# Four projection units computed block by block, convolution rows kept on chip, and tail loads issued one step ahead

## The chip, the cores and the metric

The kernel runs on one core of a Trainium2 chip. A core has TensorE (PE: matmuls into PSUM banks of 128 x 512 float32, with a separate weight-load part, PEld), VectorE (DVE), ScalarE (ACT), GpSimd (POOL) and SyncE (SP), which here only issues transfers. Each engine works off its own queue in order; an instruction that waits holds up all that stand behind it on that engine. Transfers are issued from the queues of SP, ACT and POOL. The metric is the device time of one execution in microseconds; the profile's times count from the start of the profiled span.

## The reference

One decoder layer on x of 2048 tokens by 1024 channels, float32:

```
hn   = rms_norm(x, mix_pre_g)
proj = hn @ w_in                        # q 512, k 128, v 128, u 1024 columns
a, gate = split(u)                      # 512 columns each
h    = a * sigmoid(gate)
h    = causal depthwise conv of width 31 over tokens (h) + bias
h    = silu(layer_norm(h))              # over the 512 channels
conv = h @ w_conv_pw
attn = sliding-window attention(q, k, v), window 128, sinks, position bias
x    = x + rms_norm(concat(attn, conv) @ w_out, mix_post_g)
ff   = (silu(rms_norm(x) @ w_gate) * (rms_norm(x) @ w_up)) @ w_down
out  = x + rms_norm(ff)
```

## The kernel before, in words

**Numbers.** Every float32 matmul is made of three: each operand is split into a high part (a rounded copy, made by ACT) and a low part (the rest, made by a subtraction on DVE or POOL), and `three` (L188) adds high x high, high x low and low x high. The low parts of weights are stored to a scratch tensor (`lo_in`, `lo_out`) the first time and read back for later token tiles (`split_w`, L129, argument `made`).

**Tiling.** The tokens are cut into four tiles of 512 (t = 0 to 3 in the code; tile 1 to 4 in the text). For each tile the stages are: A, the input projection, in 14 units of 128 output columns; B, attention, in blocks of 128 tokens; T, the 31 taps of the convolution on DVE; C, the tail of the convolution (transpose, layer norm, swish, transpose back); W, the output projection with its norms and residual. Then F and G compute the FFN for tiles 1 and 2 together and later for tiles 3 and 4. J multiplies `w_conv_pw` into the lower half of `w_out` once (`w_join`), so that W has eight row groups: four of attention, four of convolution.

**A projection unit.** `proj(u)` (L334) loads 512 KB of weights (all eight blocks of 128 input channels for 128 columns), splits them in two halves and runs 8 x 3 matmuls into one PSUM bank. For t = 0 the input is not normalized first: x is only scaled by its channel gain and split, and the norm's reciprocal, one number per token, is multiplied in behind the projection. It comes from `sum_squares` (ACT squares, DVE additions) and `norm_x` (four small matmuls with ones, some 13 short DVE steps, four transposes into a row `rb`). Until `rb` stands, units 0 and 1 of tile 1 hold their banks. `glu` then makes the gated product of two units, stores it to `glu_scr`, and the taps read it from there. The low parts of the weights of units 0 to 5 (`TAPS0`) are made on POOL. `FILL` and `NWARM` are matmuls on the identity that nobody reads, issued ahead of and between the first unit's.

**The convolution tail.** `stage_tail` (L594) loads four rows of 128 channels from `y_scr`, each right before its transpose, into tiles of the tag `fc`, of which there are three, shared with the taps. `conv_tail` (L609) makes mean and variance, waits a planned time (`YL`, `YL2`), scales, transposes back through the single bank `ct`, applies swish (two ACT passes, one DVE) and stores four rows to `mixT`. Stage W loads them from there (L766) and splits them.

**The order of the work.** The order is written by a planner in the code. The main stage yields an amount of planned time for each piece (5.2 for a projection unit), and lanes (`Lane`, L1333) fill in their pieces at a set rate per planned time: `lb` attention, `lc` taps (rates 0.7 for T0, 1.1 for T1), `ld` J and the tails C0 and C1 (rate 2), `lw` W0, later C2, W2, C3, W3 (rate 1.25). The taps of a channel group may be planned once its GLU store is. A scheduler then orders each engine's queue by these priorities and its own model of durations.

Of the kernel before, what the change touches and what calls it, by code (L numbers as in the profile page):

```python
# [12 lines left out]
F32 = mybir.dt.float32  # L13
# [12 lines left out]
P = 128  # L26
# [8 lines left out]


@with_exitstack
def layer_kernel(ctx, tc, x, xT, cols, rows, sinks, relb, onehot, w_in, w_pw, w_out, w_gate, w_up, w_down, out):
# [162 lines left out]
    NCOL = cols.shape[1]  # L201
    colt = cst.tile([P, NCOL], F32, name="colt")
    nc.sync.dma_start(colt, cols)
    w0 = t_("raw", (P, 2, T))
    x0 = []
    for i in range(4):
        xt = f4("x", (P, 2, T))
        for j in range(2):
            if i == 0:
                nc.sync.dma_start(w0[:, j], w_in[0, :, j * T : (j + 1) * T])  # L210
            nc.sync.dma_start(xt[:, j], xT[2 * i + j, :, 0:T])
# [116 lines left out]
    def stage_a(t, hn, before_kv, hooks, post=None):  # L328
        L = f"A{t}"
        lab[0] = L  # L330
        raw0 = [w0 if t == 0 else None]
        rb = None

        def proj(u):  # L334
            w = kweight(u, t > 0, raw0.pop() if raw0 else None)
            o = mm()
            for k in range(KC):
                three(o, [(w[k], (hn[k][:, 0], hn[k][:, 1]))], k == 0, k == KC - 1)
                for _ in range(FILL[k] if t == u == 0 else 0):
                    mat(warm[:, 0:P], ident, ident, start=True, stop=True)  # L340
            return o

        def step(u):
            if u in hooks:
# [19 lines left out]
            yield  # L364

        for c in range(4):
            og = proj(2 * c)
            if post and c == 0:
                yield 5.2
                step(0)  # L370
                late = og, proj(1)
                next(post)
                yield 5.2
                step(1)
                continue
# [7 lines left out]
            half.send(proj(2 * c + 1))  # L383
            yield 5.2
            step(2 * c + 1)
        before_kv()
# [204 lines left out]
            nc.sync.dma_start(y_scr[c, :, t * T : (t + 1) * T], y)  # L591
            yield 0.68

    def stage_tail(t):  # L594
        L = f"C{t}"
        lab[0] = L
        yt = t_("yt", (P, 4, 4 * P))
        ycs = []
        turn = turner(yt, ycs)
        for c in range(4):  # L600
            lab[0] = L
# [5 lines left out]
        yield from conv_tail(t, yt)  # L607

    def conv_tail(t, yt):  # L609
# [12 lines left out]
        for s in range(4):  # L622
            act(yt[:, s], yt[:, s], AF.Identity, scale=r[:, s : s + 1], bias=nmr[:, s : s + 1])
        for c in range(4):
            b = ct()
            for s in range(4):
                nc.tensor.transpose(b[:, s * P : (s + 1) * P], yt[:, s, c * P : (c + 1) * P], ident)
            th = f2("fc")
            act(th, b, AF.Tanh, scale=lnh[:, c : c + 1], bias=lnh[:, 4 + c : 5 + c])
            v = f2("fc")  # L630
            act(v, b, AF.Identity, scale=ln_g[:, c : c + 1], bias=ln_b[:, c : c + 1])
            stt(v, th, 1.0, v, ALU.add, ALU.mult)
            nc.sync.dma_start(mixT[4 + c, :, t * T : (t + 1) * T], v)
            yield 2
            lab[0] = L

# [108 lines left out]
    def stage_w(w, spill, G, atag, htag, mtag, bank_of, norm=None):  # L745
        L = f"W{w}"
        lab[0] = L
        acc = [f4(atag) for _ in range(4)]

        def acts(gi, ms=None):  # L750
            aa = []
            for m in ms or load(gi):
                a = hl(htag)
                act(a[:, 0], m, AF.Copy)  # L754
                vtt(a[:, 1], m, a[:, 0].bitcast(F32), ALU.subtract)
                aa.append([a])
            return aa

        stage = spare_tile() if w == 1 else None

# [12 lines left out]
            lab[0] = L  # L773
        nxt = acts(0, first)
        for gi in range(KC // G):
            aa = nxt
            for n in range(2):
                lab[0] = L
                if n == 0 and gi + 1 < KC // G:
# [4 lines left out]
                if n == 1 and gi + 1 < KC // G:  # L784
# [5 lines left out]
        tail = norm_w(w, spill, acc, mtag, gb)  # L790
        if norm:
            norm(tail)
        else:
            yield from tail

    def norm_w(w, spill, acc, mtag, gb):
        L = f"W{w}"
# [768 lines left out]
```

## Time and profile before

| | us |
|---|---|
| median of 3 runs | 1939.36 (1937.44 to 1939.98) |
| the profiled execution | 1939.64 |
| its span, first to last instruction | 1937.9 |
| TensorE busy | 1898.4 |
| VectorE busy | 1487.0 |
| ScalarE busy | 970.7 |
| GpSimd busy | 228.2 |

The page also says that 443.56 MB were moved, 229 GB/s on average, and that the granted TensorE clock was 0.994 of full speed over the span. In the views, a row names the source line, the engine, the operation and "out<-in" by the program's tile names with the stage behind the @ sign (A, B, C, F, G, H, J, W; X is the start). In brackets or behind the last bar stands how long the engine was idle before the instruction and what ended that. Most matmuls have line L108 and most DVE instructions L85, which are helpers; there the tile names tell the work. A matmul's own duration contains its latency, so PE's real pace is read from many matmuls in a row.

### The profile page before, as it was taken

The page shows a single profiled execution, that of the slowest core. Times are in us where ns is not written, and L with a number is a line of the kernel's source. Part 1 is how long each engine was busy: PE and PEld are TensorE (multiplying, and loading weights), DVE is VectorE, ACT ScalarE, POOL GpSimd, SP SyncE. Part 2 cuts the span into 40 slices and gives each one's busy share as a digit, 9 for nine tenths or more (in the row PEclk, how much of TensorE's full clock was granted, in tenths as well). Part 3 has the DMA queues.
Part 4 walks back from the last instruction along what each step waited for, and adds up shares of the span by engine and source line. Part 5 has one row for each costly group of instructions (what it writes and reads, how often), then busy time and mean ns, then how long its engine had stood idle before and what let it go on. Part 6 is the DMA issues. An engine that isn't in the chain of part 4 may idle for free.

```text
span 1937.9 us, 26778 instructions
## 1 busy us (share of the span) xinstructions
PE 1898.4 (98%) x8730; PEld 1536.7 (79%) x8730; DVE 1487.0 (77%) x2747; ACT 970.7 (50%) x1910; POOL 228.2 (12%) x327
## 2 busy tenths in 40 slices
PE   9999999999999999999999999999999999999997
PEld 7877776777778878878888778888888888888886
DVE  5999889897875899888988676787566665455557
ACT  5355444657666533334445565586534343345443
POOL 6000100221010000000000020010033333211000
PEclk9999999999999999999999999999999999999999
DMA  8897656679868676877396788699544443376664
GB/s 318 273 318 231 226 170 183 199 227 318 275 213 281 222 255 219 278 251 253 127 325 222 239 288 298 221 348 328 188 161 155 160 156 107 130 246 190 208 194 154
DMA packets 229181, 443.56 MB, mean 229 GB/s; under 512 B 22920, under 2 KB 48688, under 8 KB 229040
## 3 DMA queue, kind: packets, MB, share of 16 engines
q1 hardware_dynamic: 207408, 406.19, 63.4%
q10 hardware_dynamic: 19392, 28.32, 4.0%
q0 software_dynamic: 2240, 7.34, 1.0%
q8 instruction: 68, 1.11, 0.2%
q14 instruction: 73, 0.60, 0.1%
HBM read 320.64 MB, written 121.12 MB: 228 GB/s over the span
## 4 chain that ended last, share of the span: by engine, by line
PE 73%; DVE 10%; DMA 10%; issue 2%; ACT 2%; POOL 2%; SPq 0%; DVEq 0%; ACTq 0%; POOLq 0%
PE mm@F L108 35%; PE mm@G L108 18%; PE mm@A L108 7%; PE mm@W L108 4%; DVE fc@C L85 4%; PE tr@W L108 3%; PE tr@B L108 2%; DMA raw@A<-w_in 2%; PE ct@J L108 1%; DMA td<-fc@G 1%; DVE w@F L85 1%; PE tr@B L514 1%; DMA fc@G<-w_down 1%; DMA td<-wx@G 1%; DMA mids<-fa@F 1%
## 5 line engine op out<-in xcount | busy, mean ns | idle before, releaser
L85 DVE SCALAR_TENSOR_TENSOR fc@C<-glu@C,colt,fc@C 128x512 f32<-128x512 f32 x480 | 354.2, 754 | 2.6
L108 PE MATMUL mm@F<-hl@H,w@F 128*128 128x512 f32 x1056 | 254.2, 389 | 1.2 <-ACT mm@F L1000 1.2
L108 PEld LDWEIGHTS mm@F<-hl@H,w@F 128*128 128x128 f32 x1056 | 198.1, 188 | 42.8 <-ACT mm@F L1000 1.6
L108 PE MATMUL mm@G<-hl@G,hl@G 128*128 128x512 f32 x924 | 223.9, 393 | 1.6 <-ACT hl@G L846 1.0
L846 ACT ACTIVATE w@F<-chl@F 128x512 fp32r<-128x512 f32 x220 | 135.6, 625 | 150.5 <-PE mm@F L108 140.6
L108 PE MATMUL mm@A<-hl@A,w@A 128*128 128x512 f32 x840 | 203.7, 394 | 1.6 <-DVE hl@A L85 1.0
L108 PEld LDWEIGHTS mm@G<-hl@G,hl@G 128*128 128x128 f32 x924 | 171.7, 188 | 38.0 <-ACT hl@G L846 1.4
L108 PE MATMUL mm@G<-w@G,hl@G 128*128 128x512 f32 x876 | 199.5, 389 | 0.0
L108 PEld LDWEIGHTS mm@G<-w@G,hl@G 128*128 128x128 f32 x876 | 164.4, 188 | 34.1
L108 PEld LDWEIGHTS mm@A<-hl@A,w@A 128*128 128x128 f32 x840 | 155.8, 188 | 39.4 <-DVE hl@A L85 2.3
L85 DVE TENSOR_TENSOR w@F<-chl@F,w@F 128x512 fp32r<-128x512 f32 x198 | 146.1, 742 | 35.7 <-ACT w@F L846 35.3
L108 PE MATMUL mm@F<-ql@H,w@F 128*128 128x512 f32 x528 | 129.9, 391 | 2.6 <-ACT w@F L846 2.6
L108 PE MATMUL mm@F<-mid@H,w@F 128*128 128x512 f32 x528 | 130.7, 391 | 0.0
L108 PE MATMUL mm@F<-p@H,w@F 128*128 128x512 f32 x528 | 130.6, 393 | 0.0
L108 PE MATMUL mm@F<-x@H,w@F 128*128 128x512 f32 x528 | 128.3, 391 | 0.0
L108 PEld LDWEIGHTS mm@F<-ql@H,w@F 128*128 128x128 f32 x528 | 98.6, 188 | 23.2 <-ACT w@F L846 3.0
L108 PEld LDWEIGHTS mm@F<-p@H,w@F 128*128 128x128 f32 x528 | 100.2, 190 | 21.2 <-ACT at@F L1104 0.2
L108 PEld LDWEIGHTS mm@F<-mid@H,w@F 128*128 128x128 f32 x528 | 99.5, 189 | 21.0 <-ACT fa@F L1111 0.3
L108 PEld LDWEIGHTS mm@F<-x@H,w@F 128*128 128x128 f32 x528 | 98.4, 188 | 22.1 <-DVE mid@W L85 0.8
L133 ACT ACTIVATE w@A<-raw@A 128x512 fp32r<-128x512 f32 x110 | 67.6, 626 | 79.6 <-PE mm@A L108 50.8
L85 DVE TENSOR_TENSOR w@G<-raw@G,w@G 128x512 fp32r<-128x512 f32 x73 | 51.3, 703 | 68.5 <-ACT w@G L846 67.2
L108 PE MATMUL tr@W<-w@W,ql@W 128*128 128x512 f32 x384 | 96.9, 396 | 3.8 <-ACT ql@W L754 2.7
(307 smaller groups left out, 3185.7 us busy)
## 6 DMA issues: line engine op xcount, KB each, us to landing
mids<-fa@F SPq DMA_DIRECT2D x154, 256.0 KB, 2.8
raw@A<-w_in SPq DMA_DIRECT2D x55, 512.0 KB, 4.6
w@A<-lo_in SPq DMA_DIRECT2D x84, 256.0 KB, 3.6
fc@G<-mids SPq DMA_DIRECT2D x77, 256.0 KB, 3.4
fa@G<-mids SPq DMA_DIRECT2D x75, 256.0 KB, 5.1
w@W<-lo_out SPq DMA_DIRECT2D x48, 256.0 KB, 5.5
chl@F<-w_gate SPq DMA_DIRECT2D x22, 512.0 KB, 3.9
raw@F<-w_gate SPq DMA_DIRECT2D x22, 512.0 KB, 3.6
```

Of the source, the lines that this page charges most:

```text
L85: r = op(*args, **kw)
L108: r = nc.tensor.matmul(*args, **kw)
L133: act(w[:, 0], raw, AF.Copy)
L514: nc.tensor.transpose(o[:, i * P : (i + 1) * P], pr[:, 4 * g + i], ident)
L846: act(w[:, 0], x, AF.Copy)
```

## The change

1. *First four units.* A new input `w_four` holds the columns of units 0 to 3 by blocks of 128 input channels. For t = 0 the blocks of x and of `w_four` are loaded alternately, and `four` runs one block at a time through four banks: split on ACT and DVE, a store of the low part on POOL, twelve matmuls. The second half of the norm and the first two GLUs come behind unit 4; units 4 and 5 use banks of the tag `tr`. All low parts of input weights are made on DVE. `FILL` has 3 such matmuls instead of 11, and the bank for these matmuls is `ct`.
2. *Tiles 3 and 4.* The tail of the convolution is no longer a lane item of its own. W2 and W3 run its first half, then the attention rows, then its second half, whose rows are split on the spot (`operand`) and used by the projection; they are neither stored to nor loaded from `mixT`.
3. *Tails of tiles 1 and 2.* The load of a row is issued before the transpose of the row ahead of it, with a planned 2 behind the first.

```diff
     def kweight(u, made, raw=None):
-        hs = weight(w_in[u].rearrange("p (a b) -> p a b", a=2), lo_in[u], made, raw, u < TAPS0)
+        hs = weight(w_in[u].rearrange("p (a b) -> p a b", a=2), lo_in[u], made, raw, False)
...
     for i in range(4):
         xt = f4("x", (P, 2, T))
+        wt = f4("p", (P, 2, T))
         for j in range(2):
-            if i == 0:
-                nc.sync.dma_start(w0[:, j], w_in[0, :, j * T : (j + 1) * T])
             nc.sync.dma_start(xt[:, j], xT[2 * i + j, :, 0:T])
+            for cs in (slice(0, T // 2), slice(T // 2, T)) if i + j == 0 else (slice(0, T),):
+                nc.sync.dma_start(wt[:, j, cs], w_four[2 * i + j, :, cs])
         x0.append(xt)
+        w0 += [wt[:, 0], wt[:, 1]]
...
+        def four():
+            os = [mm() for _ in range(4)]
+            for k in range(KC):
+                lab[0] = L
+                w = hl("w")
+                for cs in (slice(0, T // 2), slice(T // 2, T)) if k == 0 else (slice(0, T),):
+                    act(w[:, 0, cs], w0[k][:, cs], AF.Copy)
+                    vtt(w[:, 1, cs], w0[k][:, cs], w[:, 0, cs].bitcast(F32), ALU.subtract)
+                nc.gpsimd.dma_start(
+                    lo_in[0:4, k // 4, :, k % 4 * P : (k % 4 + 1) * P].rearrange("u p c -> p u c"),
+                    w[:, 1].bitcast(F32).rearrange("p (u c) -> p u c", c=P))
+                for u in range(4):
+                    us = slice(u * P, (u + 1) * P)
+                    three(os[u], [((w[:, 0, us], w[:, 1, us]), (hn[k][:, 0], hn[k][:, 1]))], k == 0, k == KC - 1)
+                for _ in range(FILL[k]):
                     mat(warm[:, 0:P], ident, ident, start=True, stop=True)
+                if k == KC - 2:
+                    next(post)
+                yield 2.7
+                if k % 2:
+                    step(k // 2)
+            return os
...
         for c in range(4):
-            og = proj(2 * c)
             if post and c == 0:
-                yield 5.2
-                step(0)
-                late = og, proj(1)
-                next(post)
-                yield 5.2
-                step(1)
+                os = yield from four()
+            if post and c < 2:
                 continue
-            if post and c == 1:
+            og = proj(2 * c, tr if post and c == 2 else mm)
+            if post and c == 2:
                 rb = next(post)
-                next(glu(0, *late))
+                for j in range(2):
+                    next(glu(j, *os[2 * j : 2 * j + 2]))
...
+        if t < 2:
+            row(0)
+            yield 2
         for c in range(4):
-            y = f2("fc")
-            nc.sync.dma_start(y, y_scr[c, :, t * T : (t + 1) * T])
-            ycs.append(y)
+            row(c + (t < 2))
             turn(c)
             yield 0.5
...
             stt(v, th, 1.0, v, ALU.add, ALU.mult)
-            nc.sync.dma_start(mixT[4 + c, :, t * T : (t + 1) * T], v)
+            if sink:
+                sink(v)
+            else:
+                nc.sync.dma_start(mixT[4 + c, :, t * T : (t + 1) * T], v)
...
+        def operand(m):
+            a = hl(htag)
+            act(a[:, 0], m, AF.Copy)
+            vtt(a[:, 1], m, a[:, 0].bitcast(F32), ALU.subtract)
+            return [a]
...
+        conv = []
+        tail = stage_tail(w, lambda v: conv.append(operand(v))) if w > 1 else ()
+        for y in tail:
+            if y == YL2:
+                break
+            yield y
...
         for gi in range(KC // G):
-            aa = nxt
+            if w > 1 and G * gi == 4:
+                yield from tail
+                lab[0] = L
+            aa = nxt if w < 2 or G * gi < 4 else conv[G * gi - 4 : G * gi - 4 + G]
...
-    FILL = (2, 2, 2, 2, 2, 1, 0, 0)
+    FILL = (1, 1, 1, 0, 0, 0, 0, 0)
...
-    warm = mm()
+    warm = ct()
...
-    lw.add("C2", stage_tail(2))
     lw.add("W2", stage_w(2, True, 2, "mid", "ql", "at", tr))
-    lw.add("C3", stage_tail(3), lambda: since(lc, "T3", CS))
-    lw.add("W3", stage_w(3, True, 2, "mid", "ql", "at", tr, norm=lambda g: lw.add("N3", g)))
+    lw.add("W3", stage_w(3, True, 2, "mid", "ql", "at", tr, norm=lambda g: lw.add("N3", g)),
+           lambda: since(lc, "T3", CS))
```

More of the change, by code (lines that the diff above doesn't have):

```diff
@@ L37, in layer_kernel @@
 @with_exitstack
-def layer_kernel(ctx, tc, x, xT, cols, rows, sinks, relb, onehot, w_in, w_pw, w_out, w_gate, w_up, w_down, out):
+def layer_kernel(ctx, tc, x, xT, cols, rows, sinks, relb, onehot, w_in, w_four, w_pw, w_out, w_gate, w_up, w_down, out):
     nc = tc.nc
@@ L330, in stage_a, with proj @@
         lab[0] = L
[L331 removed]
         rb = None
[L334 to L336 removed]
+        def proj(u, bank_of=mm):
+            w = kweight(u, t > 0)
+            o = bank_of()
             for k in range(KC):
                 three(o, [(w[k], (hn[k][:, 0], hn[k][:, 1]))], k == 0, k == KC - 1)
[L339 to L341 removed]
+            return o
+        def four():
[13 more added lines that the diff above has]
+                for _ in range(FILL[k]):
+                    mat(warm[:, 0:P], ident, ident, start=True, stop=True)
+                if k == KC - 2:
[4 more added lines that the diff above has]
+            return os
         def step(u):
@@ L382, in stage_a @@
             step(2 * c)
-            half.send(proj(2 * c + 1))
+            half.send(proj(2 * c + 1, tr if post and c == 2 else mm))
             yield 5.2
@@ L599, in stage_tail, with row, conv_tail @@
         turn = turner(yt, ycs)
+        def row(c):
+            if c < 4:
+                lab[0] = L
+                ycs.append(f2("fc"))
+                nc.sync.dma_start(ycs[c], y_scr[c, :, t * T : (t + 1) * T])
+        if t < 2:
+            row(0)
+            yield 2
         for c in range(4):
-            lab[0] = L
-            y = f2("fc")
-            nc.sync.dma_start(y, y_scr[c, :, t * T : (t + 1) * T])
-            ycs.append(y)
+            row(c + (t < 2))
             turn(c)
             yield 0.5
-        yield from conv_tail(t, yt)
-    def conv_tail(t, yt):
+            lab[0] = L
+        yield from conv_tail(t, yt, sink)
+    def conv_tail(t, yt, sink):
         L = f"C{t}"
@@ L748, in stage_w @@
         acc = [f4(atag) for _ in range(4)]
-        def acts(gi, ms=None):
[L751 to L757, printed above, removed]
+        def operand(m):
[3 more added lines that the diff above has]
+            return [a]
+        def acts(gi, ms=None):
+            return [operand(m) for m in ms or load(gi)]
+        conv = []
[4 more added lines that the diff above has]
+            yield y
+        lab[0] = L
         stage = spare_tile() if w == 1 else None
@@ L775, in stage_w @@
         for gi in range(KC // G):
-            aa = nxt
+            if w > 1 and G * gi == 4:
+                yield from tail
+                lab[0] = L
+            aa = nxt if w < 2 or G * gi < 4 else conv[G * gi - 4 : G * gi - 4 + G]
             for n in range(2):
                 lab[0] = L
-                if n == 0 and gi + 1 < KC // G:
+                more = gi + 1 < KC // G and (w < 2 or G * gi + G < 4)
+                if n == 0 and more:
                     if w < 2 and G * gi + G == 4:
@@ L783, in stage_w @@
                     rows_next = load(gi + 1)
-                if n == 1 and gi + 1 < KC // G:
+                if n == 1 and more:
                     nxt = acts(gi + 1, rows_next)
@@ L789, in stage_w @@
                 yield from block_half(acc, list(zip(aa, ws)), n, gi == 0, L, bank_of)
-        tail = norm_w(w, spill, acc, mtag, gb)
+        last = norm_w(w, spill, acc, mtag, gb)
         if norm:
-            norm(tail)
+            norm(last)
         else:
-            yield from tail
+            yield from last
     def norm_w(w, spill, acc, mtag, gb):
@@ L1551 @@
         ("w_in", kblocks(wi)),
+        ("w_four", cc(wi[:, 0 : 4 * P].reshape(KC, P, 4 * P))),
         ("w_pw", cc(wp)),
```

5 lines of the change are left out of this document (2 added, 3 removed).

## The prediction

> **What bounds the kernel now.** I read the page's first lines, then the stretches of time, then the groups and waits of the stretches that the change touches.
>
> ```profile
> span 1937.9 us, 26778 instructions
> PE 1898.4 (98%) x8730; PEld 1536.7 (79%) x8730; DVE 1487.0 (77%) x2747; ACT 970.7 (50%) x1910; POOL 228.2 (12%) x327
> ```
>
> TensorE (PE) is the bound: it is idle for 39.5 us of 1937.9, and a change that leaves its matmuls alone can gain only from that idle time, from half-clock time, and from stretches in which PE counts as busy but issues few matmuls. The view of stretches shows where these lie (columns: stretch, its length, then busy time and number of instructions of PE, PEld, DVE, ACT, POOL, then granted clock, DMA share, GB/s).
>
> ```profile
> 0.00:5.00 5.00, 3.35 (x15) 3.35 (x16) 0.54 (x7) 1.91 (x2) 1.20 (x8) 1.00 0.50 122
> 5.00:10.00 5.00, 4.34 (x29) 3.63 (x27) 1.50 (x2) 2.90 (x4) 3.85 (x4) 1.00 1.00 305
> 10.00:15.00 5.00, 4.40 (x17) 2.91 (x17) 4.74 (x9) 4.75 (x8) 0.00 (x0) 1.00 1.05 404
> 15.00:20.00 5.00, 4.62 (x20) 3.30 (x19) 4.64 (x4) 3.25 (x5) 3.94 (x4) 1.00 1.03 415
> 20.00:40.00 20.00, 18.58 (x87) 15.08 (x86) 11.93 (x26) 10.77 (x18) 12.89 (x17) 1.00 0.86 313
> 40.00:60.00 20.00, 20.00 (x86) 15.43 (x85) 16.31 (x28) 4.89 (x9) 12.33 (x18) 1.00 0.89 296
> 60.00:200.00 140.00, 137.99 (x679) 108.44 (x678) 136.07 (x297) 77.32 (x183) 8.22 (x16) 1.00 0.81 275
> 200.00:260.00 60.00, 57.23 (x299) 44.03 (x298) 49.73 (x115) 23.51 (x64) 9.63 (x4) 1.00 0.63 208
> 1060.00:1070.00 10.00, 7.57 (x37) 5.80 (x35) 6.36 (x10) 4.37 (x8) 0.00 (x0) 1.00 0.70 213
> 1070.00:1080.00 10.00, 9.67 (x35) 7.59 (x36) 9.69 (x16) 6.42 (x12) 0.00 (x0) 0.83 0.46 138
> ```
>
> Three things are to be seen. The first 20 us issue only 81 PE instructions while the DMA rings are full from 5 us on. From 60 to 200 us PE and DVE are both full (138.0 and 136.1 of 140): there DVE is almost a second bound. At 1060 to 1080 PE stands still for 2.8 us and then runs at a lower clock.
>
> **Part 1, the first four units together.** Now unit 0 waits, block by block, for all of x, and each later unit waits for its own 512 KB of weights. The groups of the first 40 us:
>
> ```profile
> L108 PE MATMUL mm@A<-hl@A,w@A 128*128 128x512 f32 x110 | 28.1, 402 | 1.6 <-DVE hl@A L85 1.0 <-ACT hl@A L319 0.6
> L135 POOL TENSOR_TENSOR w@A<-raw@A,w@A 128x512 fp32r<-128x512 f32 x9 | 11.9, 1339 | 12.9 <-ACT w@A L133 12.8
> L85 DVE TENSOR_TENSOR gb@A<-gb@A,wx@A 128x512 f32<-128x512 f32 x6 | 8.8, 1463 | 1.7 <-ACT wx@A L283 1.5
> L108 PE MATMUL mm@X<-ident 128*128 128x128 f32 x40 | 7.2, 347 | 1.6 <-POOL ident masks.py:199 1.6
> L133 ACT ACTIVATE w@A<-raw@A 128x512 fp32r<-128x512 f32 x10 | 5.9, 624 | 3.3 <-DMA raw@A<-w_in 3.3
> L85 DVE SCALAR_TENSOR_TENSOR hl@A<-x@X,colt,hl@A 128x512 fp32r<-128x512 f32 x8 | 5.7, 748 | 5.4 <-ACT hl@A L319 5.4
> L319 ACT ACTIVATE hl@A<-x@X,colt 128x512 fp32r<-128x512 f32 x8 | 5.3, 711 | 2.0 <-DMA x@X<-xT 2.0
> L108 PE MATMUL ct@A<-ones,gb@A 128*128 128x1 f32 x8 | 0.9, 239 | 0.0
> L283 ACT ACTIVATE wx@A<-x@X 128x1024 f32<-128x1024 f32 x4 | 4.2, 1049 | 4.0 <-DVE gb@A L85 4.0
> ```
>
> and from the timeline, in order, PE, ACT and SP:
>
> ```profile
> 31.33 11.61 PE L108 MATMUL mm@A<-hl@A,w@A 128*128 128x512 f32 x50
> 4.31 0.63 ACT L133 ACTIVATE w@A<-raw@X 128x512 fp32r<-128x512 f32 x1 [2.22 <-DMA raw@X<-w_in]
> 6.19 0.72 ACT L319 ACTIVATE hl@A<-x@X,colt 128x512 fp32r<-128x512 f32 x1 [1.25 <-DMA x@X<-xT]
> 8.46 0.72 ACT L319 ACTIVATE hl@A<-x@X,colt 128x512 fp32r<-128x512 f32 x1 [0.77 <-DMA x@X<-xT]
> 1.73 0.42 SPq L211 DMA_DIRECT2D x@X<-xT  x1
> 2.67 3.78 SPq L211 DMA_DIRECT2D x@X<-xT  x7
> ```
>
> At full pace a matmul takes 11.61/50 = 0.23 us, a unit of 24 5.5 us. 110 are done by 40 us, so the 96 of four units end at 40 - 14 x 0.23 = 36.8 us.
>
> After: each step k needs 256 KB of x and 256 KB of weights and gives PE 12 matmuls, 2.75 us. The rings moved 0.61 MB by 5 us, 2.13 MB by 10 us and 4.15 MB by 15 us (5 x 122, 305, 404 GB/s). Step 0 with its constants is 0.6 MB, step 1 ends at 1.1 MB (6.7 us), step 7 at 4.3 MB (15.3 us). Landing is seen later than moving: the second x block stood at 1.1 MB of what was issued and was used at 8.46, so I add 1.7 us. Step 0 can start at about 6.2 (first operand used at 6.19), step 1 at 8.4 plus one ACT and one DVE pass over x, 8.4 + 0.71 + 0.75 = 9.9; step 7's data are there by 17 us, when PE is at step 3. From step 1 PE is the limit: 9.9 + 7 x 2.75 + 0.9 (the sums' ones matmuls) = 30.0 us. ACT gives 0.71 + 0.62 + 0.52 (half a square) = 1.85 us a step. DVE gives 0.75 for x, and for the low part of the weights and the sum two tensor_tensor, each 0.74 by this row of the page:
>
> ```profile
> L85 DVE TENSOR_TENSOR w@F<-chl@F,w@F 128x512 fp32r<-128x512 f32 x198 | 146.1, 742 | 35.7 <-ACT w@F L846 35.3
> ```
>
> 2.23 us, also under 2.75. The sums stand at 1463 ns now, twice that, because they ran beside POOL's splits; these leave POOL. **Gain 36.8 - 30.0 = 6.8 us.** At best step 1 starts right behind step 0 (9.0): 7.7. At worst each in-order step waits once as now (0.5 us a step): 2.8.
>
> The rest of part 1. SP issues 18 transfers instead of 10 ahead of x of the next tile, 8.5 us at 0.47 each, before the last byte is due. Fewer fillers (24 of today's 40 records) cost nothing if PE waits no longer than 0.9 us at step 1. POOL issues eight stores of the low parts instead of the splits and is free for it; their pieces are shorter (512 B), which no row prices: 0 if they land at leisure (tile 2 reads them after 90 us), up to 1 us if the rings, full until 20 us, are slowed. I take 0. The banks of units 0 to 3 stay held until the norm is there, but units 4 and 5 use three other banks, so the first taken bank is wanted 11 us after step 7; each pair is read in two DVE passes of 0.75 with one of 0.62 on ACT between, 4 us for both pairs behind a norm that stands behind unit 4 (5.5). I take 0, at worst 2.
>
> **Part 2, what DVE pays.** Units 4 and 5 are split on DVE, 4 x 0.74 = 3.0 us, where 60 to 200 us is full. The taps of the convolution start when the first GLU is stored; the planner now reaches it after 21.6 + 5.2 units of its clock instead of 15.6 (10.4 relative to the end of tile 1). On the chip the first tap stood at
>
> ```profile
> 44.30 0.54 DVE L85 TENSOR_SCALAR fc@C<-glu@C,colt 128x512 f32<-128x512 f32 x1
> 463.70 0.32 SPq L766 DMA_DIRECT2D mb@J<-mixT  x1
> 472.12 1.31 ACT L754 ACTIVATE hl@W<-mb@J 128x512 fp32r<-128x512 f32 x2 [2.03 <-PE mm@A L108]
> DMA to landing us min/median/max: 2.3/4.8/7.9
> ```
>
> which is 13 us behind the norm (unit 4's matmuls start behind its transposes, at 31.33). Now the norm's transposes stand behind unit 4, 30.0 + 5.5, and POOL, with no splits ahead of the GLU's last product, saves one pass of 1.3: 47.2. With PE 6.8 us ahead, taps and splits are 6.8 + 2.9 + 3.0 = 12.7 us later against PE. 200 to 260 us has 10.3 us of DVE idle time to make that up. Who would wait is the projection of tile 2 for its convolution rows: they were loaded at 463.70 (landed about 468.5, median 4.8) and used at 472.12 behind PE, 3.6 us of slack. **Cost taken: 1.5 us**; ends 0 (all made up) and 9.1 (12.7 less the slack); it lies near the low end, since idle time and slack together, 13.9, cover the slip.
>
> **Part 3, rows of tiles 3 and 4 on chip.** Sixteen transfers of 256 KB go (eight stores, eight loads). What they cost at 1060 to 1090:
>
> ```profile
> ACT ql@W L754 <- DMA at@W<-mixT: 17.8, 3, 8.9
> PE tr@W L108 <- ACT ql@W L754: 2.7, 1, 2.7
> 1070.33 3.81 PE L108 MATMUL tr@W<-w@W,ql@W 128*128 128x512 f32 x9 [2.69 <-ACT ql@W L754]
> ```
>
> ACT stands before the load up to 8.9 us, and PE once for 2.7; behind it the clock is 0.83 for 10 us, 1.7 us more. 4.4 us in all. The copies and subtractions stay. Next late is the conv tail itself (ACT, DVE, one bank), which runs while the attention rows' matmuls and the other lane feed PE. **Gain 4.0**; ends 4.4 and -1.0 (a new wait of 2.7 us at both tiles). The planner's wait of 20 units goes too, so both tiles end earlier, which nobody waits for.
>
> A rule weighed here: the Trainium skill, TensorE: Matmul & The Clock Gate, Part 1, lets the clock fall only after an idle window of about 3.4 us. By it the 2.7 us wait costs no clock and this part would gain 2.7 instead of 4.4; this trace disagrees, with 0.83 behind a wait of 2.69 us.
>
> **Part 4, tails of tiles 1 and 2.** The one wait seen:
>
> ```profile
> 399.47 0.66 PE L575 MATMUL ct@C<-ident,fc@C 128*128 128x128 f32 x4 [1.67 <-DMA fc@C<-y_scr]
> ```
>
> The row is now issued about a step earlier. **Gain 1.0**; ends 1.7 and 0 (three buffers, still one behind the taps).
>
> **Sum.** 6.8 - 1.5 + 4.0 + 1.0 = 10.3 us. The profiled execution took 1939.64 (span 1937.9 and 1.7 around it), 0.3 above the median 1939.36 of the three runs: 1929.3, so 1929.0 on the median.
>
> **Rivals.** *The start is fed no better*: ACT and DVE take their work in an order in which PE waits at each step. For it: PE waited on both for 1.6 us of unit 0's 24 matmuls; against: 2.75 us of matmuls per step now cover what 0.7 did not. Gain 2.8 instead of 6.8 and the DVE cost half: 1933; with two more us lost on the held banks 1935.
>
> *The conv tail stalls PE in place of the load*: -1.0 instead of 4.0, 1934. For it: one bank and four passes over ACT and DVE per row; against: ACT is half idle there (4.4 and 6.4 of 10).
>
> *Slower: the late taps starve the projection of tile 2.* If the taps follow the planner's clock and not free DVE time, 10.4 units later is much more on the chip: from 320 to 460 us tile 4's projections got
>
> ```profile
> L108 PE MATMUL mm@A<-mid@A,w@A x132: 387/389/628, 320.9 to 459.7; 128*128 128x512 f32 x132
> L108 PE MATMUL mm@A<-hl@A,w@A x126: 387/389/504, 319.8 to 459.9; 128*128 128x512 f32 x126
> ```
>
> 258 matmuls, 10.75 units of 5.2 in 140 us, 2.5 us each, so up to 26 us. Less 3.6 of slack PE waits 22: 1939.4 - 11.8 + 22 = 1950. It decides once the slip is over 11.8 + 3.6 = 15.4 us. Against: DVE's 10.3 us of idle time, and a slip by its own work of 12.7 us.
>
> The Trainium skill's clock rule (same page) speaks against fewer fillers: a window without matmuls halves the clock. By the sum the longest wait at the start is 0.9 us, so I give it no case.
>
> **How the numbers follow.** My case 0.58 (1924 to 1933 by its own ends); start no better 0.15 (half of it inside 0.2%); conv stall 0.12; starved projection 0.15. A measurement tells about 0.2%, 3.9 us, from no change. Faster: 0.58 + 0.12 + 0.08 = 0.78, same 0.07, slower 0.15. The range 1921 to 1938 leaves out the slow rival and a little of my own case below: ends of 7.7, 0, 4.4 and 1.7 give 1925.6, and waits elsewhere that move with the new order may take or give some 4 us.
>
> **What would show it.** Right: 96 matmuls of the first units done near 30 us; tile 1's projections ending 6 to 7 us earlier; no ACT wait on loads of mixT after 900 us and PE without a wait over 1 us at 1040 to 1100, clock 1.00; no wait of ct@C on y_scr. Wrong: PE waiting near 460 to 530 us on the convolution rows of tile 2, a clock below 1 in the first 30 us, or new PE waits on ql@W.

## The result, and the profile after

| | before | after |
|---|---|---|
| median | 1939.67 (6 runs, 1935.90 to 1945.08) | 1958.46 (6 runs, 1951.05 to 1959.09) |
| ratio, 95% interval | | 1.0073 (1.0055 to 1.0091) |
| profiled execution, span | 1939.64, 1937.9 | 1959.09, 1957.3 |
| granted TensorE clock | 0.994 | 0.990 |

Slower by 0.7%, 14 us, by the ratio on record, in which the experiments below are given too (the two medians alone are 18.8 us apart). 10 us less had been forecast: 1929.0, in a range of 1921 to 1938. On other chips the median of the kernel before lay between 1942 and 1946, so the experiments are given as ratios to its runs on the same chip.

The first lines of the page, after:

```profile
span 1957.3 us, 26728 instructions
PE 1904.8 (97%) x8714; PEld 1539.7 (79%) x8714; DVE 1490.0 (76%) x2760; ACT 971.6 (50%) x1911; POOL 206.9 (11%) x311
```

TensorE is busy for 6 us more although it has 16 matmul records less, which is time at half clock, and it is idle for 13 us more (52.5 against 39.5). DVE has 3 us more work in sum: thirteen more passes for low parts of weights (some 9.4 us, since those of units 0 to 3 came to DVE too, not only the four of units 4 and 5 that the prediction put down as a load), against 4.6 us less in the norm's six sums. POOL has 21 us less.

The stretches of time, after (columns as in the prediction):

```profile
10.00:15.00 5.00, 5.00 (x23) 4.14 (x23) 4.21 (x8) 4.95 (x8) 1.95 (x3) 1.00 1.05 402
15.00:20.00 5.00, 5.00 (x23) 4.13 (x23) 5.00 (x9) 4.10 (x7) 1.83 (x3) 1.00 1.05 397
20.00:40.00 20.00, 20.00 (x95) 16.32 (x94) 9.74 (x31) 9.10 (x16) 2.68 (x8) 1.00 1.03 400
40.00:60.00 20.00, 18.01 (x68) 13.38 (x67) 14.39 (x25) 6.17 (x11) 5.53 (x12) 0.91 0.83 278
60.00:200.00 140.00, 130.97 (x641) 103.94 (x640) 124.89 (x281) 71.52 (x175) 9.54 (x16) 0.98 0.74 251
200.00:260.00 60.00, 60.00 (x303) 46.31 (x302) 52.65 (x119) 26.16 (x69) 5.09 (x4) 1.00 0.67 212
385.00:450.00 65.00, 60.25 (x304) 45.71 (x301) 55.15 (x132) 34.99 (x84) 12.15 (x24) 0.97 0.67 207
450.00:640.00 190.00, 180.19 (x870) 139.74 (x869) 131.14 (x288) 121.51 (x254) 20.30 (x56) 0.97 0.76 259
1060.00:1070.00 10.00, 10.00 (x47) 8.28 (x46) 6.12 (x12) 4.19 (x9) 0.00 (x0) 1.00 0.62 193
1070.00:1080.00 10.00, 10.00 (x46) 8.27 (x45) 7.68 (x19) 5.49 (x10) 3.75 (x12) 1.00 0.70 210
```

The two ends of the change look as forecast: from 10 to 40 us PE is full at clock 1.00, and the wait at 1067 us is gone. The loss lies between them. From 60 to 200 us, PE issues 38 instructions fewer than before (641 against 679), although DVE, the second bound there, is busy for 11 us *less* (124.9 against 136.1). From 385 to 640 us PE loses more, against these rows of before:

```profile
385.00:450.00 65.00, 63.33 (x320) 47.43 (x319) 55.51 (x126) 39.16 (x92) 13.22 (x34) 1.00 0.73 226
450.00:640.00 190.00, 185.78 (x925) 146.76 (x924) 149.61 (x317) 132.09 (x276) 17.62 (x47) 1.00 0.80 271
```

Busy time is 3.1 + 5.6 us less, and a clock of 0.97 in place of 1.00 over these 255 us costs some 7.7 us more: 16 us in all. I counted the matmuls of the projections in the traces and set the end of each unit (24 matmuls; 14 units a tile; the end is the start of the last one plus 0.23 us) side by side:

| end of unit | before | after | difference |
|---|---|---|---|
| 4 | 36.9 | 30.4 | -6.5 |
| 7 | 54.0 | 51.4 | -2.6 |
| 25 | 169.7 | 165.2 | -4.5 |
| 28 | 189.3 | 196.0 | +6.8 |
| 48 | 391.5 | 396.7 | +5.2 |
| 50 | 425.1 | 435.7 | +10.5 |
| start of the third row group of H | 616.8 | 637.8 | +21.0 |

So the front's gain is there and is given back twice over: 11 us at the step from tile 2 to tile 3 (units 25 to 28), and 16 us between 390 and 640 us. PE's own waits name the places; after, the five largest of 0 to 190 us, then all of 385 to 430 us:

```profile
PE mm@A L108 <- DVE ql@A L85: 4.7, 1, 4.7
PE mm@A L108 <- DVE w@A L85: 1.8, 1, 1.8
PE tr@B L108 <- POOL p@B L535: 1.7, 1, 1.7
PE ct@X L108 <- POOL ident masks.py:199: 1.7, 1, 1.7
PE tr@B L108 <- DVE sm@B L490: 1.4, 1, 1.4
```

```profile
PE ct@C L593 <- ACT yt@C L594: 3.1, 1, 3.1
PE mm@W L108 <- DVE x@W L85: 1.1, 1, 1.1
PE ct@C L593 <- DMA fc@C<-y_scr: 0.6, 1, 0.6
```

The first row is the largest: at 176 us PE waits 4.7 us for DVE to empty the bank of a q row.

### The profile page after: what moved, and what is told of

It is laid out like the page before. It is cut to its first block, busy times and chain, and to the rows that moved or that the text cites. A ratio compares the mean times of both kernels' runs of the same rounds, so it can differ in the third digit from the quotient of the medians.

```text
span 1957.3 us, 26728 instructions
## 1 busy us (share of the span) xinstructions
PE 1904.8 (97%) x8714; PEld 1539.7 (79%) x8714; DVE 1490.0 (76%) x2760; ACT 971.6 (50%) x1911; POOL 206.9 (11%) x311
## 4 chain that ended last, share of the span: by engine, by line
PE 64%; DVE 17%; DMA 12%; issue 3%; ACT 3%; SPq 1%; POOL 1%; DVEq 0%; ACTq 0%; POOLq 0%
PE mm@F L108 32%; PE mm@G L108 20%; DVE fc@C L85 6%; PE mm@A L108 4%; PE tr@W L108 4%; PE mm@W L108 2%; DMA raw@A<-w_in 1%; DMA x@A<-xT 1%; DMA mids<-fa@F 1%; DVE w@F L85 1%; DMA chl@F<-w_gate 1%; DMA glu@C<-glu_scr 1%; DVE chl@F L85 1%; PE tr@B L108 1%; DVE fa@F L85 1%
## 5 line engine op out<-in xcount | busy, mean ns | idle before, releaser
L108 PE MATMUL mm@A<-hl@A,w@A 128*128 128x512 f32 x792 | 193.2, 396 | 2.9 <-DVE w@A L85 1.8
L108 PEld LDWEIGHTS mm@A<-hl@A,w@A 128*128 128x128 f32 x792 | 147.8, 189 | 37.3 <-issue 2.5
L133 ACT ACTIVATE w@A<-raw@A 128x512 fp32r<-128x512 f32 x104 | 63.6, 625 | 87.6 <-PE mm@A L108 43.5
L108 PE MATMUL mm@W<-w@W,hl@W 128*128 128x512 f32 x384 | 101.3, 408 | 5.4 <-ACT mid@W L755 2.9
```

What stands on the lines that cost most here:

```text
L108: r = nc.tensor.matmul(*args, **kw)
L133: act(w[:, 0], raw, AF.Copy)
```

## The experiments

**Each part alone.** The edits are the change's own hunks, one part at a time, on the kernel before; the fourth kernel has only the fewer fillers.

```diff
-    FILL = (2, 2, 2, 2, 2, 1, 0, 0)
+    FILL = (1, 1, 1, 0, 0, 0, 0, 0)
```

> The kernel before with the first part alone (four units block by block, their banks, the splits of units 4 and 5 on DVE, fewer fillers); conv rows and tails as before. Theory A (the whole loss is an after-effect of the first part: weights of units 4 to 6 late, DVE's queue fuller, taps late): 8 to 20 us slower than before, with the half-clock stretches near 46 and 179 us in its trace as in the changed kernel. Theory B (the loss comes from the other two parts' new queues): 3 to 7 us faster than before, as the front's gain is kept. Theory C (any new order of the scheduled queues moves the time by several us): anything between -7 and +15, with the gaps at other places than in the changed kernel.

> The kernel before with the conv rows of tiles 3 and 4 handed on in SBUF, and nothing else. Theory A: 2 to 5 us faster (the wait of 2.69 us near 1068 and the lower clock behind it gone, no ACT wait on mixT there), nothing changed before 900 us. Theory B: 3 to 8 us slower. Theory C: nothing is moved before 900 us either way, since the scheduled queues up to there hold the same work.

> The kernel before with the loads of the tails of tiles 1 and 2 a step ahead, and nothing else. Theory A: -2 to +1 us, and the 1.67 us wait of ct@C on y_scr near 399 us gone. Theory B: 4 to 8 us slower, with new gaps at 400 to 500 us as in the changed kernel (3.06 us near 407, 2.92 us near 491). Theory C: +-4 us, with gaps elsewhere.

> The kernel before with fewer filler matmuls in unit 0 (1,1,1,0,0,0,0,0 in place of 2,2,2,2,2,1,0,0), and nothing else: 8 matmuls of 128x128 are left out. Theories A and B: within 1 us of before, clock 1.00 in the first 40 us. Theory C: several us either way with gaps at places far behind the start (above 2 us from before would be a sign that a mere new order costs that much).

| kernel | ratio to before | 95% interval |
|---|---|---|
| front alone | 0.9990 | 0.9974 to 1.0005 |
| conv rows alone | 0.9970 | 0.9954 to 0.9986 |
| tails alone | 1.0006 | 0.9990 to 1.0021 |
| fewer fillers alone | 0.9959 | 0.9943 to 0.9975 |

No part costs anything by itself, so theories A and B both fall (and the fewer fillers speak for C, that a new order alone moves the time); the sum of the three, some -7 us, stands against +14. The front alone has the same 4.7 us wait at 176 us (unit 25 at -3.2, unit 28 at +5.7), and so gains only 2 us, where its own terms promised 5.3; of the 9 us lost at that step it has 4.5 back by unit 56 (+1.2). It doesn't lose anything at 390 to 640 us. The fewer fillers gained 8 us, which nobody had forecast; I come back to that.

**Two parts at a time, and two versions.** The changed kernel without its conv part; without its tails; the latter with the splits of units 4 and 5 on POOL again; and, on the kernel before, conv part and fewer fillers together.

```diff
-        hs = weight(w_in[u].rearrange("p (a b) -> p a b", a=2), lo_in[u], made, raw, False)
+        hs = weight(w_in[u].rearrange("p (a b) -> p a b", a=2), lo_in[u], made, raw, u < TAPS0)
```

> The changed kernel with the conv rows of tiles 3 and 4 going through mixT again: the first part and the tails' prefetch together. Theory D (the loss is made by these two together: with the taps late against TensorE, the prefetched rows of a tail stand in SP's queue, waiting for a buffer, ahead of the loads of conv rows that the projection of tile 1 wants near 400 us): 12 to 22 us slower than before, with a PE wait of about 3 us near 407 us. Rival E (each part's cost adds: -2 and +1 us were measured alone): within 3 us of before. Rival F (the loss needs the third part): within 5 us of before.

> The changed kernel without the tails' prefetch. Theory D: the loss goes; the sum of the two parts measured alone, -2 and -6 us, so 5 to 10 us faster than before. Rival F: 8 us slower than before or more.

> As the kernel with the first part and the conv part, but the low parts of units 4 and 5 are subtracted on POOL as before, which frees DVE of four passes of 0.7 us. Theory G (the front's 6 us are given back near 154 to 184 us because DVE is short of time by what the change loaded on it): 2 to 6 us faster than the same kernel with the splits on DVE, the wait of 4.7 us near 176 us shorter by 2 us or more. Rival H (DVE isn't short of time but stands behind loads of the convolution's input, 7 us in 50 to 180 us): within 2 us of it, and the wait near 176 us stays over 3.5 us.

> The kernel before with the conv rows of tiles 3 and 4 on chip and the fewer fillers, without the new front and the tails' prefetch. If the two single gains of -6 and -8 us are real and add: 1928 to 1933 where before is 1944, 11 to 15 us faster. If the gain with fewer fillers was a chance of the order: 4 to 8 us faster.

| kernel | ratio to before | 95% interval |
|---|---|---|
| front + tails | 1.0066 | 1.0042 to 1.0089 |
| front + conv | 0.9977 | 0.9964 to 0.9990 |
| front + conv, splits on POOL | 1.0013 | 0.9995 to 1.0031 |
| conv + fewer fillers | 0.9946 | 0.9926 to 0.9965 |

Front and tails together make the whole second loss; the conv part has no share in it. The conv part and the fewer fillers together were 10 us faster, a little less than the sum of the two. Theory G falls: with four passes, 3 us, less on DVE the wait at 176 us was 6.0 us, not shorter. Its rival H had the wait right, but the whole was 7 us slower than with the splits on DVE (1.0013 against 0.9977), which H didn't allow; why is open. What DVE does there is seen in its waits; first before, then after (both 50 to 180 us):

```profile
DVE w@A L85 <- ACT w@A L133: 1.1, 1, 1.1
DVE fc@C L85 <- DMA glu@C<-glu_scr: 1.1, 1, 1.1
DVE gb@A L85 <- POOL sm@A L162: 0.9, 1, 0.9
```

```profile
DVE fc@C L85 <- DMA glu@C<-glu_scr: 5.8, 2, 3.0
DVE fa@A L85 <- PE mm@A L108: 3.8, 1, 3.8
DVE ql@A L85 <- ACT ql@A L439: 2.5, 1, 2.5
DVE mb@X L740 <- PE tr@X L108: 1.1, 1, 1.1
DVE gb@A L85 <- POOL sm@A L162: 0.5, 1, 0.5
```

DVE stands still for 13.7 us in these rows instead of 3.1, with everything queued behind whatever waits, and then meets the step to tile 3 with the taps that were queued ahead of it still to do.

**Where the prefetched row waits.** The tails of the first tile in SP's queue (start, duration of the issue), front + conv, then the changed kernel:

```profile
287.49 0.32 SPq L609 DMA_DIRECT2D y_scr<-fc@C  x1
290.27 0.32 SPq L621 DMA_DIRECT2D fc@C<-y_scr  x1
301.22 0.32 SPq L621 DMA_DIRECT2D fc@C<-y_scr  x1
307.60 0.32 SPq L621 DMA_DIRECT2D fc@C<-y_scr  x1
```

```profile
289.97 0.32 SPq L609 DMA_DIRECT2D y_scr<-fc@C  x1
292.85 0.32 SPq L622 DMA_DIRECT2D fc@C<-y_scr  x1
327.02 0.32 SPq L609 DMA_DIRECT2D y_scr<-fc@C  x1
331.03 0.32 SPq L622 DMA_DIRECT2D fc@C<-y_scr  x1
```

The second row, which was to come a step *earlier*, comes 30 us later: in SP's order it stands behind the store, at 327 us, of the taps' accumulator that held its buffer. Four kernels tell what makes it so; a fifth, with the taps at a lower rate, belongs to the first loss.

One row ahead only:

```diff
         for c in range(4):
-            row(c + (t < 2))
+            if t > 1:
+                row(c)
             turn(c)
+            if t < 2:
+                row(c + 1)
```

The prefetch in the tail of tile 1 only (for tile 2: t == 1):

```diff
-        if t < 2:
+        if t == 0:
             row(0)
...
-            row(c + (t < 2))
+            row(c + (t == 0))
```

The pause taken out, and the other rate of the taps (on front + conv):

```diff
             row(0)
-            yield 2
...
-    RC0, RC1, RC2, RC3, RW0, RW, RB, LC = 0.7, 1.1, 0.4, 0.9, 1.7, 1.25, 0.8, 100
+    RC0, RC1, RC2, RC3, RW0, RW, RB, LC = 0.6, 1.1, 0.4, 0.9, 1.7, 1.25, 0.8, 100
```

> The changed kernel with the tails of tiles 1 and 2 holding one row at a time again: the first row is still loaded early, but row c+1 is asked for only behind the turn of row c. Theory K (the prefetch makes a tail hold two of the three fc buffers, so its second row waits for the one that a taps' accumulator holds, some 30 us: in the changed kernel row 1 of the first tail was loaded at 331 us, behind the store of the accumulator at 327 us, where the kernel without prefetch loaded it at 301 us): the loss goes, 3 to 8 us faster than before (as without prefetch), and the row is loaded near 301 us. Rival L (it is the earlier start of the tail, or its yield of 2, that shifts the order): 8 to 20 us slower than before, as the changed kernel.

> The changed kernel with the prefetch in the tail of tile 1 only. Theory K (the harm is done where the first tail's second row waits for a buffer): 8 to 18 us slower than before, most of the change's loss. Rival M (the harm is in the second tail, whose rows stand in SP's queue ahead of the projection's loads near 400 us): 3 to 8 us faster than before.

> The changed kernel with the prefetch in the tail of tile 2 only. Theory K: 1 to 7 us faster than before. Rival M: 8 us slower or more.

> The kernel with the first and the conv part, without prefetch, with the taps of tile 1 handed out at a rate of 0.6 in place of 0.7. Theory I (what gives the front's 6 us back near 176 us is DVE's queue in order: taps put ahead of the splits and of the q rows of the next tile by a planner that thinks DVE is on time): the wait of 4.7 us near 176 us falls below 2 us and unit 30 ends 4 us or more earlier against the same kernel at 0.7; the whole 0 to 5 us faster than it. Rival N (DVE is simply full up to there; the order doesn't matter): the wait stays above 3.5 us, the whole within 2 us or slower, since later taps come late for the tails.

> The changed kernel without the pause (yield 2) behind the first row of a tail; two rows are still loaded ahead. Theory L (the pause lets the planner place a taps' accumulator ahead of the second row, which is then given that accumulator's buffer): the second row of the first tail loads near 301 us, 2 to 8 us faster than before. Theory K (holding two of three buffers is enough): the row still loads near 330 us, 8 to 18 us slower than before.

| kernel | ratio to before | 95% interval | second row of the first tail loaded at |
|---|---|---|---|
| one row ahead only | 1.0050 | 1.0036 to 1.0063 | 328.1 |
| prefetch in the tail of tile 1 only | 1.0038 | 1.0019 to 1.0057 | 332.1 |
| prefetch in the tail of tile 2 only | 0.9979 | 0.9962 to 0.9997 | 300.7 |
| changed kernel without the pause | 0.9975 | 0.9962 to 0.9988 | 300.8 |

Most of the harm is done in the first tail, and it goes with the pause alone: two held buffers (theory K) are not what matters, as the kernel with one row ahead still waits and the one without the pause doesn't. SP's waits before the tails' loads from 286 to 350 us name the releaser, changed kernel first, then without the pause (in total, times, longest):

```profile
SPq L622 <- DMA y_scr<-fc@C: 4.7, 2, 3.2
SPq L622 <- DMA fc@C<-y_scr: 3.2, 1, 3.2
SPq L622 <- PE ct@C L593: 0.7, 1, 0.7
```

```profile
SPq L622 <- PE ct@C L593: 9.7, 3, 4.5
SPq L622 <- DMA y_scr<-fc@C: 1.4, 1, 1.4
```

Without the pause three of the four rows are released by the transpose of the row before, exactly as in the kernel without any prefetch: nothing is loaded ahead at all, for want of a free buffer. With the pause the next row has the accumulator's buffer. SP itself stands still for that store only 4.7 us, in two waits, and issues a dozen other transfers between the two rows: most of the 30 us are the row's place in the order. That the pause lets the planner put the end of that accumulator ahead of the row is what I infer; the releasers and the times are measured. What follows is read off the changed kernel's trace, step by step, and was not tested singly: the stores of the first tail end at 396 us instead of 375 in front + conv, the projection's load of them leaves SP at 402.18 instead of 395.55, ACT stands before it with the copy of the next tail's transposes queued behind, and PE with it:

```profile
402.18 0.93 SPq L802 DMA_DIRECT2D fa@W<-mixT  x2
...
407.06 0.63 ACT L780 ACTIVATE hl@W<-fa@W 128x512 fp32r<-128x512 f32 x1 [6.47 <-DMA fa@W<-mixT]
409.17 0.63 ACT L780 ACTIVATE hl@W<-fa@W 128x512 fp32r<-128x512 f32 x1 [1.48 <-DMA fa@W<-mixT]
409.70 0.58 ACT L594 ACTIVATE yt@C<-ct@C 128x512 f32<-128x512 f32 x1
...
410.34 0.66 PE L593 MATMUL ct@C<-ident,fc@C 128*128 128x128 f32 x4 [3.06 <-ACT yt@C L594]
```

This chain doesn't explain the loss by itself. In before the stores end at 394 us and the last load leaves at 399.62, with the tails' part alone at 396 and 401.30, and that kernel loses less than 2 us between 390 and 620 us. What the runs show is that front and pause together make it: in the five kernels that have both, the second row comes 38 to 40 us behind the first and the ratio is 1.0038 to 1.0114; in those with the front but without a pause in the first tail it comes 7 to 22 us behind, and the ratio is 1.0013 at most. How the late row becomes 16 us between 390 and 640 us stays open beyond the one wait of 3.06 us.

The Trainium skill, Perfetto Trace Analysis, section Identifying Performance Opportunities, has the same gap repeating on the engine that should be busy as a possible sign that buffers are too few. This trace agrees as to the cause only: here a load was late for want of a free buffer, and PE had no repeating gap but single waits under other names.

**The rate of the taps.** Of theory I, the kernel with the front, the conv part and the taps at 0.6 (expectation above) gave the answer; three more put it to the test.

> The changed kernel, all parts, with the taps of tile 1 at a rate of 0.6 in place of 0.7. If both losses come from taps that the planner places earlier than DVE gets to them: both go, 14 to 22 us faster than before as the kernel without prefetch was at 0.6 (0.990). If the prefetch harms by itself: 0 to 10 us faster than before.

> The kernel before with the taps of tile 1 at 0.6, and nothing else. Theory I (the rate mends a harm that the new front made): within 4 us of before, since before has no wait there to mend. Rival O (0.6 is a better rate for any front): 8 us faster than before or more, and the front is worth little.

> The first and the conv part without prefetch, the taps of tile 1 at 0.65. Theory I: between the two rates measured, a wait of 1 to 4 us near 176 us, 6 to 16 us faster than before. If the gain at 0.6 is a chance of one order: anything from 8 us slower to 4 us faster than before, with the wait of 4.7 us still there.

| kernel | taps' rate | wait near 176 us | unit 28 against before | ratio to before | 95% interval |
|---|---|---|---|---|---|
| front + conv | 0.7 | 4.7 | +4.1 | 0.9977 | 0.9964 to 0.9990 |
| front + conv | 0.65 | 3.2 | -0.4 | 0.9987 | 0.9972 to 1.0001 |
| front + conv | 0.6 | none | -7.4 | 0.9901 | 0.9881 to 0.9922 |
| before | 0.6 | none | +2.3 | 1.0020 | 1.0005 to 1.0036 |
| all parts, with the pause | 0.6 | none | -6.6 | 1.0114 | 1.0082 to 1.0145 |

Theory I holds: the wait goes as the rate goes down, and the front then keeps its 6 to 7 us. Without the new front the lower rate gains nothing. On before's trace it does bring units 42 to 56 forward (+3.8 to -3.8 us against before), but that is lost again behind them, in PE waits of 3.6 and 2.5 us between 490 and 565 us and at a clock of 0.81 from 502 to 520 us. At 0.65 the wait was smaller, as theory I has it, but the whole was only 2.5 us faster, as its rival has it; new waits came up between 490 and 530 us (3.0 and 2.0 us). The groups of taps on DVE ahead of the q row that PE waits for, before up to 177.5 us, changed kernel up to 179.9 us and the rate 0.6 up to 167 us, show what moved (count, then min/median/max ns):

```profile
L85 DVE SCALAR_TENSOR_TENSOR fc@C<-glu@C,colt,fc@C x94: 704/748/1785, 45.4 to 169.2; 128x512 f32<-128x512 f32 x94
```

```profile
L85 DVE SCALAR_TENSOR_TENSOR fc@C<-glu@C,colt,fc@C x88: 694/743/1122, 56.3 to 178.5; 128x512 f32<-128x512 f32 x88
```

```profile
L85 DVE SCALAR_TENSOR_TENSOR fc@C<-glu@C,colt,fc@C x72: 737/744/752, 54.4 to 146.6; 128x512 f32<-128x512 f32 x72
```

At the lower rate sixteen taps of 0.74 us, 12 us, stand behind the splits and the q row instead of ahead of them, and DVE gets to the q row 13 us earlier than in the changed kernel. But more taps ahead isn't what the change brought: before had 94 and hardly a wait (0.5 us). What is new in the changed kernel is that DVE stood still longer on its way, and reached the row 4.4 us later than in before (179.98 against 175.56), while PE came earlier; the lower rate makes room for both. The wait for loads of the convolution's input falls from 5.8 to 0.6 us, and the stretch of the step is full, first front + conv at 0.7, then at 0.6:

```profile
154.00:190.00 36.00, 29.64 (x145) 22.45 (x144) 30.29 (x77) 18.03 (x45) 4.04 (x3) 0.91 0.51 164
```

```profile
154.00:190.00 36.00, 36.00 (x183) 27.88 (x183) 35.15 (x77) 24.57 (x56) 2.20 (x3) 1.00 0.78 250
```

The lower rate doesn't mend the tails' pause. The changed kernel got worse with it, which neither of the two forecasts allowed. Its second row stood behind an accumulator again (first row 269.1, second 308.7 us; without the pause 268.8 and 290.6). At unit 56 it is still 8.0 us ahead of before; it falls behind between 475 and 565 us, where PE's longest wait, 5.8 us, is before a transpose of a convolution tail.

**Both mended.** All three parts, without the pause and with the taps at 0.6; and front + conv at 0.6 once more.

> All three parts, without the pause behind a tail's first row and with the taps of tile 1 at 0.6. If the two losses are two separate things and both are mended: 0.987 to 0.993 of before, as the front and conv part at 0.6. If the second row is given an accumulator's buffer in this order too (the row then loads over 25 us behind the first turn): 1.000 or more.

> The first and the conv part with the taps at 0.6, once more beside other runs of before, since its interval rested on four runs: 0.988 to 0.993 of before.

They took 0.9920 (0.9901 to 0.9939) and 0.9924 (0.9903 to 0.9945) of before, medians 1928.4 and 1928.2 where before had 1941.95. Each loss has its own mending of one number, and the tails' prefetch, once harmless, gives nothing. The two are not independent, though: with the pause kept, the lower rate makes the whole slower, 1.0114 against 1.0073. The version with all three parts and both mendings beats both kernels.

## Why the prediction was wrong, by its own steps

**Part 1, gain 6.8: right against this trace of before, 6.5.** Four units end at 30.4 us (forecast 30.0). That the gain agrees so closely is partly luck. With the conv rows alone, the tails alone and before at the lower rate, the start has the same order of instructions as in before, and there the four units end at 41.7, 41.2 and 40.5 us instead of 36.9; with the new front they end between 30.4 and 31.1 in every trace. So the gain lies between 6 and 11 us by the trace of before that is taken. PE's rows, after:

```profile
6.95 19.36 PE L108 MATMUL mm@A<-hl@A,w@A 128*128 128x512 f32 x84 [0.86 <-ACT w@A L347]
27.55 3.01 PE L108 MATMUL mm@A<-hl@A,w@A 128*128 128x512 f32 x12
```

84 matmuls in one go: step 1's wait of 0.9 us didn't come, the start was 0.7 us later instead. "Fewer fillers cost nothing" was right for the start, but taking them out alone gained 8 us. Between 300 and 345 us that kernel's trace lacks a wait of 3.1 us of before and the low clock behind it (0.92 there, 1.00 in this kernel), yet it has new waits at 476 us, and its profiled execution was no faster than that of before. Why the median gains is open; what the traces show is that the order of PE's instructions differs from before's from 43 us on, though only matmuls that nobody reads were taken out.

**"The banks stay held ... I take 0": wrong by 1 to 4 us.** Unit 7 was only 2.6 us ahead; units 5 to 7 took 21.0 us instead of 17.1 (18.1 to 20.7 in the other traces with this front). The bank was not late; DVE was: with the four units' GLU passes and a wait for the next tile's row norms in its queue it came to the split of the next weights at 42.8 us, PE waited 1.77 us, and 3.4 us at half clock followed. This is read from the trace; no run tested it.

**Part 2, cost 1.5: the step that failed first.** At the step to tile 3 it measured 11 us. The slip of the taps was larger than forecast: the first stood at 55.8 us against 44.3, 11.5 us later instead of 2.9, since its input left SP only at 47.9 us; with PE 2.6 to 4.5 us ahead and 3.0 us of splits that makes 17 to 19 us, not 12.7. But what failed above all is "covered by idle time at 200 to 260 us and the slack of tile 2's projection": the taps share DVE's in-order queue with the splits and q rows of the next projection tile, so the first one to wait isn't the projection at 460 us but PE at 176 us, ahead of all that cover. The rival of late taps had the right cause and a wrong place; it was to decide from a slip of 15.4 us, which was passed, and had 0.15. The prediction added up DVE's work and left out the time in which DVE stands still (13.7 us from 50 to 180 us, against 3.1 before); what makes each of these waits longer was not tested singly. Sixteen taps fewer ahead of the step, 12 us, mend the wait; four passes fewer on DVE, 3 us, did not.

**Part 3, gain 4.0: right alone, less in the changed kernel.** Alone 0.3% (0.14 to 0.46), 2.7 to 8.9 us; PE's order is that of before up to 1007 us there, so the gain isn't a new order ahead of it. The wait at 1067 us is gone, and PE is full at clock 1.00 from 1060 to 1080 us. But in the changed kernel a like wait stands at 1018 us, 2.72 us for ACT with 3.4 us at clock 0.54 behind it: between the last matmul of the first F (975.7 us in before) and the first of the second (1387.0) it makes up 2.5 us, conv rows alone 4.1.

**Part 4, gain 1.0, ends 1.7 and 0: the step that failed second, and the costlier one.** Alone it is within the measurement of zero; with the front it costs 0.8% (1.0066 against 0.9990), with front and conv part 1.0% (1.0073 against 0.9977). The prediction saw the reason, "three buffers, still one behind the taps", and used it to bound the gain at 0. It should have bounded the loss: a load that is given a buffer held by a serial chain comes behind that chain, here 30 us later, and the rest of its tail with it. The wait that was to go is gone with this part alone, but in the changed kernel PE waited 2.5 us for rows of `y_scr`, in before 1.7. No row was quoted for how long an accumulator lives, though the trace of before has it: two first passes at 251.28 us, and the first store behind them at 300.46.

**The sum of 10.3 us** lies near what the kernel with both faults mended gains, 13.6 us, but not for the reasons of its terms. Part 4 gives nothing, and of the 14.0 us that this kernel is ahead at unit 56, 9 come between units 42 (4.9 ahead) and 56, which no term of the sum had; before at the lower rate makes 7.6 us there too. The range was also narrower than its own ends: with every part at its worst, 2.8 - 9.1 - 1.0 + 0, the kernel is 7.3 us slower, 1946.7, and the prediction left that out together with the rival that came nearest.

## What to carry to other kernels

Work that is moved earlier on the bound engine moves nothing on the others: ask, for the first hand-over behind it, what already stands in the other engines' queues ahead of what that hand-over needs, and pace the filler work to it. A prefetch needs a free buffer at the time of the load; count who holds each buffer of the tag and for how long, and if a serial chain holds one, a load that is given it is not early but as late as the chain. Test parts in pairs: here each was harmless alone.

## What was not expected of the hardware

TensorE's clock fell behind short waits, in stretches of one length. In the changed kernel, behind waits of 1.77 and 4.71 us:

```profile
45.80:49.20 3.40, 3.40 (x10) 2.62 (x9) 2.01 (x4) 0.00 (x0) 1.28 (x1) 0.50 1.01 230
178.90:185.70 6.80, 5.03 (x12) 3.96 (x13) 4.36 (x16) 0.00 (x0) 0.00 (x0) 0.50 1.01 372
```

and in the kernel before, behind a wait of 2.77 us, not at all:

```profile
212.00:215.00 3.00, 0.24 (x2) 0.00 (x0) 1.88 (x3) 0.23 (x1) 2.96 (x2) 1.00 0.61 232
215.00:218.40 3.40, 3.39 (x23) 1.78 (x24) 1.14 (x3) 0.60 (x1) 0.00 (x0) 1.00 0.00 0
```

A short wait thus cost 1.7 us beside itself (half of 3.40), or 2.5 (half of the 5.03 us in which PE was busy; the rest of that stretch was the wait itself), or nothing, and its length doesn't tell which. The Trainium skill, TensorE: Matmul & The Clock Gate, Part 1, has a freely running window of 3413 ns that decides, and the stretches of 3.4 and 6.8 us agree with it; that it takes a whole idle window doesn't, since 1.77 us halved the clock here.
